# Pooling-group products as three part products, with weights and columns split in the tile's modulation room

## The chip, the cores and the metric

The kernel runs on one core of a Trainium2 chip. The core's engines each work through a queue of their own, in order: TensorE (PE) multiplies, VectorE (DVE) and ScalarE (ACT) work elementwise, GpSimd (POOL) does the same and is almost unused here, SyncE (SP) issues nearly all DMAs. They wait for one another by semaphores. The metric is the device time of one execution in microseconds; lower is better.

## The reference, cut to what matters

One inference step of a two-layer encoder. 1024 prompt rows and 32 sample rows of 1024 channels go through layer 0 (a gating mixer, then a channel MLP, "ffn0") and layer 1 (a pooling mixer, then a channel MLP, "ffn1"). Each half is wrapped in RMS norms, a modulation `rmsnorm(x) * (1 + scale) + shift` and a gated residual. The changed part is the linear map of the pooling mixer:

```python
pooled = jnp.concatenate(outs, axis=-1) - hf[:, L - n_out:]      # window means minus identity
pooled = pooled.astype(h_ext.dtype).reshape(bsz, n_out, POOL_GROUPS, POOL_GROUP_DIM)
y = jnp.einsum('btgc,gcd->btgd', pooled, w_grp).reshape(bsz, n_out, D_MODEL)
return y * scale
```

There are four groups of 256 channels; each has a 256 x 256 matrix. All data are float32.

## The kernel before, in words

Activations lie transposed: 128 channels on the partitions, eight blocks `k` of them, the rows as columns. The rows are cut into three tiles `t` of 384, 384 and 288 columns (the third holds 256 prompt and the 32 sample rows). `acc[t]` is a tile's running array; the residual stream is kept in DRAM (`xd`).

Almost all large products are made of part products. A float32 operand is split in two: `split` (line 1167) writes a first part in the format float32r with ACT (a copy, line 1168) and the rest with DVE (the subtraction runs through the wrapper of line 79). `products` (line 911) then issues three float32r matmuls per pair, first x first, first x second and second x first (lines 916 to 918). Weights stream through three `raw` buffers; ACT writes their first part (line 439) and DVE their second. The products of the pooling groups are the exception: line 1580 multiplies float32 operands directly, `wg` as loaded and `acc` as it is.

A modulated tile is kept as `hh[t]` (first part, ACT, line 889) and `hl[t]` (second part, DVE). Each has one room per tile, tag `h<part><t>`, made by `room` (line 132). The room `hh` of a tile is free between the last up product of ffn0 for that tile and its next modulation, that for ffn1.

The order of the work is written by a planner. `run_ffn` walks through `passes`, a list of (layer, chunk, tiles). In each, `ffn_item` issues four up products per tile (PSUM names `pf`) and later eight down products (`pg`), which DVE adds to `acc`; the first chunk's are copied there by ACT. Between the products `weave` (line 708) streams weights and pulls steps out of `fillers`, generators with the work between two halves of a layer. A step is pulled while the planner's count of DVE time is behind its count of PE time (`tick`, and the wrappers of line 79). What a generator yields says when it may go on: `False` at once, `True` at once and ahead of others, a number only when PE's count has passed the present one by so many microseconds. `pull` looks at the first two fillers. Before the first chunk of a tile, `finish` pulls until that tile's filler is empty, whatever the counts say.

For layer 1 the filler `ffn1_t` (in `to_pool`, line 1445) does, in order: residual and norm behind ffn0; modulation in place; for the third tile the loads and transposes of the cache, and the transposes of the pooling state (`stT`, line 1511), which DVE copies out (`stp`, line 1514); the window sums (`win`) on DVE; then per group a pause, the load of `wg` on SP, four matmuls into two PSUM buffers `pp`, eviction by ACT (line 1584) and squares for the next norm; last `mix_to_ffn` with `residual`, the norm (`pn_r1_1_t`, line 805, with the factors `r` and `q`) and `modulate`. ffn1 runs all of chunks 0 to 3 for the first tile, then for the second, then for the third.

When the kernel is built, the instructions of each engine are put into a fixed order; that order can differ from the one in which the code issued them, and it can be read from the build of either kernel. The engines keep to it.

Of the kernel before, what the change touches and what calls it, by code (L numbers as in the profile page):

```python
# [9 lines left out]
F32 = mybir.dt.float32  # L10
F32R = mybir.dt.float32r
AF = mybir.ActivationFunctionType
ALU = mybir.AluOpType
AX = mybir.AxisListType

P = 128
# [18 lines left out]
def tile_stream_encoder_step(  # L35
# [25 lines left out]
    nc = tc.nc  # L61
    act = nc.scalar.activation
    mm = nc.tensor.matmul
# [5 lines left out]
    def tick(us):  # L69
        time["pe"] += us  # L70
        time["dve"] = max(time["dve"], time["pe"] - 4.0)
# [16 lines left out]
    def pool(name, **kw):  # L88
        return ctx.enter_context(tc.tile_pool(name=name, bufs=1, reuse_waits="tile", **kw))
# [27 lines left out]
        out=quad, in_=ident.rearrange("p (c m) -> p m c", m=32), op=ALU.add, axis=AX.X  # L117
# [9 lines left out]
    def A(t, kb, c0=0, w=None):  # L127
        w = ncol[t] - c0 if w is None else w
        return acc[t][:, kb, HALO + c0 : HALO + c0 + w]


    def room(part, t, name, dtype=F32):
        return work.tile([P, KB, ncol[t]], dtype, tag=f"h{part}{t}", bufs=1, name=name)
# [4 lines left out]
    def ps_dn(name):  # L138
        return psum.tile([P, 512], F32, tag="pd", bufs=3, name=name)

    def ps_ms(name):
        return psum.tile([P, 512], F32, tag="pm", bufs=3, name=name)
# [18 lines left out]
    def t_x(name, shape):  # L161
        return work.tile(shape, F32, tag="x3", bufs=3, name=name)
# [748 lines left out]
    def products(ps, n, terms):  # L911

        last = len(terms) - 1
        tick(3 * len(terms) * (0.004 + n / 2265.0))
        for i, (wh, wl, rh, rl) in enumerate(terms):
            mm(ps[:, :n], wh, rh, start=i == 0, stop=False)  # L916
            mm(ps[:, :n], wh, rl, start=False, stop=False)  # L917
            mm(ps[:, :n], wl, rh, start=False, stop=i == last)  # L918
# [99 lines left out]
    with tc.manual_schedule():  # L1018
# [65 lines left out]
        ps = ps_ms("pv0_5")  # L1084
# [41 lines left out]
    for p, b in v_order:  # L1126
        ps = ps_dn(f"pv{p}_{b}")
# [39 lines left out]
    def split(dst_hi, dst_lo, src, n):  # L1167
        act(out=dst_hi[:, :n], in_=src[:, :n], func=AF.Copy)  # L1168
        tt(out=dst_lo[:, :n], in0=src[:, :n], in1=dst_hi[:, :n].bitcast(F32), op=ALU.subtract)
# [270 lines left out]
    late = pool("late")  # L1440
# [4 lines left out]
    def to_pool(st):  # L1445
        t = st.t
        n = ncol[t]
        npr, nsm = TILES[t][1], TILES[t][2]

        def run():  # L1450
            need_ada(0, 5)
            out = []
# [5 lines left out]
            if nsm:  # L1458
                ext = t_m("ext")
                pool_ext["e"] = ext.rearrange("p (k c) -> p k c", k=KB)  # L1460
                for half in range(2):
# [3 lines left out]
                    for i in range(4):  # L1465
                        k = half * 4 + i
# [9 lines left out]
            for k in range(KB):  # L1476
                for c0, w, v in segs[t]:
                    a = A(t, k, c0, w)
                    stt(
                        out=a,  # L1480
                        in0=a,
                        scalar=coef[:, 1, 0, v, k : k + 1],
                        in1=r[:, c0 : c0 + w],
# [5 lines left out]
                        out=dst,  # L1489
                        in_=a,  # L1490
                        func=AF.Identity,
# [26 lines left out]
            parts = [(acc[t][:, :, 0 : HALO + npr], npr, 0, "p")]  # L1518
            if nsm:
                parts.append((pool_ext["e"], nsm, npr, "s"))  # L1520
            for src, w, dst0, nm in parts:
                for g in range(4):
# [3 lines left out]
                    for lev in range(g + 1):  # L1526
# [3 lines left out]
                            out=nxt[:, :, lo:],  # L1530
                            in0=cur[:, :, lo:],
                            in1=cur[:, :, lo - step : HALO + w - step],
                            op=ALU.add,
# [9 lines left out]
                    if first:  # L1543
                        tt(
                            out=cur[:, :, HALO : HALO + win],
                            in0=cur[:, :, HALO : HALO + win],
                            in1=inv[:, 0:win].unsqueeze(1).broadcast_to([P, 2, win]),
                            op=ALU.mult,
                        )
                        tt(  # L1550
                            out=dst[:, :, 0:win],
                            in0=cur[:, :, HALO : HALO + win],
                            in1=hsrc[:, :, 0:win],
                            op=ALU.subtract,
# [3 lines left out]
                        out=dst[:, :, o:],  # L1558
                        in0=body[:, :, o:],
                        scalar=1.0 / win,  # L1560
                        in1=hsrc[:, :, o:],
# [3 lines left out]
                    yield g != 3  # L1565

            sp = Stat(t, f"rp_{t}")
            for g in range(4):
                yield 0.5
                tick(8 * (0.01 + n / 1220.0))  # L1570
                if g % 2 == 0:
                    wg = t_x(f"wg{t}_{g}", [P, 2, 256])
                else:
                    wg = late.tile([P, 2, 256], F32, tag="wg", bufs=1, name=f"wg{t}_{g}")
                nc.sync.dma_start(wg, pool_w_grp[0, g].rearrange("(k p) d -> p k d", p=P))
                pss = []
                for e in range(2):
                    ps = ps_dn(f"pp{t}_{g}_{e}")
                    for k in range(2):
                        mm(ps[:, :n], wg[:, k, e * P : (e + 1) * P], A(t, 2 * g + k), start=k == 0, stop=k == 1)  # L1580
                    pss.append(ps)
                for e in range(2):
                    d = 2 * g + e
                    act(out=A(t, d), in_=pss[e][:, :n], func=AF.Copy, scale=pscale[:, d : d + 1])
                    sp.square(d)
            yield from mix_to_ffn(sp, 1)

        fillers.append((f"ffn1_{t}", run()))

    def run_ffn(l, after):  # L1590
# [130 lines left out]
```

## Time and profile before

| | |
|---|---|
| time, median of 3 runs | 2165.97 us (2165.47 to 2168.23) |
| the profiled execution's own time | 2166.51 us |
| its span, first to last instruction | 2164.7 us |
| busy: PE, DVE, ACT, POOL | 2147.6, 1421.0, 985.6, 8.0 us |
| pooling products (line 1580), first and last start | 1233.9 and 1565.4 us |
| granted TensorE clock, mean | 0.998 |

The profiled execution is 0.5 us longer than the median of the runs. In the profile a row of a timeline gives start, duration, engine, line and operation with output and inputs, and behind it, where the engine stood idle, for how long and what ended that. In rows of grouped instructions the columns are count, busy time, mean duration in ns, and idle time before them with what ended it. A row of waits gives total, number and longest. A row of a stage gives its length and for each engine the busy time, then the granted clock, the DMA share and GB/s. Durations of matmuls overlap, so the pace of PE is read from their starts. A float32 matmul shows as two passes.

### The profile page before, as it was taken

How to read it: one execution, taken by the hardware profiler on the slowest of the kernel's cores; microseconds unless marked ns; L12 is line 12 of the kernel's file. 1: busy time of each engine (PE TensorE's matmuls, PEld its weight loads, DVE VectorE, ACT ScalarE, POOL GpSimd, SP SyncE). 2: the span in 40 equal slices, each digit the busy share in tenths (PEclk: the TensorE clock that was granted, in tenths of full speed). 3: DMA queues.
4: the chain of work that ended last, by engine and by line, in shares of the span. 5: the costliest groups of instructions: out<-in, count | busy, mean ns of one | idle time of the engine just before them, and what ended most of it. 6: DMA issues, size and time to landing. Idle time of an engine off the chain costs nothing.

```text
span 2164.7 us, 33237 instructions
## 1 busy us (share of the span) xinstructions
PE 2147.6 (99%) x13238; PEld 2082.7 (96%) x13238; DVE 1421.0 (66%) x2517; ACT 985.6 (46%) x1673; POOL 8.0 (0%) x20
## 2 busy tenths in 40 slices
PE   8999999999999999999999999999999999999998
PEld 6878999999999999999999999999999999999998
DVE  6787738467778549576757779869675553523375
ACT  5634322233456652324445566666564542322354
POOL 0000000000000000000000000000000000000000
PEclk9999999999999999999999999999999999999999
DMA  8486524353446444334545466464454541302342
GB/s 296 156 267 210 168 81 135 93 155 103 137 126 218 129 147 146 98 117 140 181 125 164 147 188 202 146 191 156 141 182 134 162 151 59 107 20 69 100 127 108
DMA packets 354864, 312.97 MB, mean 145 GB/s; under 512 B 10834, under 2 KB 316538, under 8 KB 354708
## 3 DMA queue, kind: packets, MB, share of 16 engines
q1 hardware_dynamic: 354452, 310.61, 45.9%
q8 instruction: 104, 1.70, 0.3%
q14 instruction: 52, 0.43, 0.1%
q10 hardware_dynamic: 128, 0.14, 0.0%
q0 software_dynamic: 128, 0.09, 0.0%
HBM read 278.95 MB, written 31.84 MB: 144 GB/s over the span
## 4 chain that ended last, share of the span: by engine, by line
PE 98%; ACT 1%; DMA 0%; DVE 0%; issue 0%; POOL 0%; POOLq 0%; SPq 0%; ACTq 0%; DVEq 0%
PE pf L916 11%; PE pf L918 11%; PE pf L917 11%; PE pg L916 11%; PE pg L918 11%; PE pg L917 11%; PE pu L916 3%; PE pu L918 3%; PE pu L917 3%; PE po L916 3%; PE po L918 3%; PE po L917 3%; PE pv L942 2%; PE pv L944 2%; PE pv L943 2%; PE psp L1262 1%
## 5 line engine op out<-in xcount | busy, mean ns | idle before, releaser
L916 PE MATMUL pg<-fh,wh_dn 128*128 128x384 f32 (+1 forms) x1536 | 496.1, 323 | 0.0
L916 PE MATMUL pf<-hh,wh_up 128*128 128x384 f32 (+1 forms) x1536 | 494.4, 322 | 0.0
L917 PE MATMUL pf<-hl,wh_up 128*128 128x384 f32 (+1 forms) x1536 | 493.1, 321 | 0.0
L918 PE MATMUL pf<-hh,wl_up 128*128 128x384 f32 (+1 forms) x1536 | 493.0, 321 | 0.0
L917 PE MATMUL pg<-fl,wh_dn 128*128 128x384 f32 (+1 forms) x1536 | 492.5, 321 | 0.0
L918 PE MATMUL pg<-fh,wl_dn 128*128 128x384 f32 (+1 forms) x1536 | 492.5, 321 | 0.0
L79 DVE TENSOR_TENSOR wl_up<-raw,wh_up 128x1024 fp32r<-128x1024 f32 x152 | 186.0, 1225 | 170.0 <-ACT wh_up L439 170.0
L916 PEld LDWEIGHTS pg<-fh,wh_dn 128*128 128x128 f32 x1536 | 288.3, 188 | 1.3 <-ACT fh L1168 0.4
L917 PEld LDWEIGHTS pg<-fl,wh_dn 128*128 128x128 f32 x1536 | 288.3, 188 | 1.0 <-DVE fl L79 0.2
L918 PEld LDWEIGHTS pf<-hh,wl_up 128*128 128x128 f32 x1536 | 288.6, 188 | 0.6 <-DVE wl_up L79 0.6
L439 ACT ACTIVATE wh_up<-raw 128x1024 fp32r<-128x1024 f32 x152 | 161.1, 1060 | 280.3 <-PE pf L917 217.2
L917 PEld LDWEIGHTS pf<-hl,wh_up 128*128 128x128 f32 x1536 | 288.3, 188 | 0.4
L916 PEld LDWEIGHTS pf<-hh,wh_up 128*128 128x128 f32 x1536 | 288.2, 188 | 0.4
L918 PEld LDWEIGHTS pg<-fh,wl_dn 128*128 128x128 f32 x1536 | 288.3, 188 | 0.0
L79 DVE TENSOR_TENSOR acc<-acc,pg 128x384 f32<-128x384 f32 (+1 forms) x336 | 174.3, 519 | 154.7 <-PE pg L918 154.1
L439 ACT ACTIVATE wh_dn<-raw 128x1024 fp32r<-128x1024 f32 x152 | 161.0, 1060 | 209.9 <-PE pg L917 174.0
L79 DVE TENSOR_TENSOR wl_dn<-raw,wh_dn 128x1024 fp32r<-128x1024 f32 x152 | 186.1, 1224 | 82.5 <-ACT wh_dn L439 82.2
L79 DVE SCALAR_TENSOR_TENSOR aa<-raw,csil,aa 128x512 f32<-128x512 f32 (+1 forms) x364 | 203.6, 624 | 6.7 <-DMA raw<-in_w_ada_dram 6.3
L1344 ACT ACTIVATE r<-pf 128x384 f32<-128x384 f32 (+1 forms) x192 | 86.6, 451 | 199.3 <-PE pf L918 190.3
L79 DVE TENSOR_TENSOR fl<-r,fh 128x384 fp32r<-128x384 f32 (+1 forms) x192 | 100.4, 523 | 87.2 <-ACT fh L1168 85.8
L916 PE MATMUL pu<-hh,wh_u 128*128 128x384 f32 (+1 forms) x384 | 125.9, 328 | 0.0
L916 PE MATMUL po<-ush,wh_o 128*128 128x384 f32 (+1 forms) x384 | 123.5, 322 | 0.0
(270 smaller groups left out, 2931.7 us busy)
## 6 DMA issues: line engine op xcount, KB each, us to landing
raw<-in_ffn_w_up_dram SPq DMA_DIRECT2D x152, 512.0 KB, 3.9
raw<-in_ffn_w_down_dram SPq DMA_DIRECT2D x152, 512.0 KB, 3.3
raw<-in_w_ada_dram SPq DMA_DIRECT2D x96, 512.0 KB, 4.3
raw<-in_sgu_w_in_dram SPq DMA_DIRECT2D x40, 512.0 KB, 4.1
xd<-acc SPq DMA_DIRECT2D x8, 1536.0 KB, 7.4
raw<-in_sgu_w_out_dram SPq DMA_DIRECT2D x24, 512.0 KB, 3.9
xo_r<-xd SPq DMA_DIRECT2D x32, 384.0 KB, 3.4
vd<-vt SPq DMA_DIRECT2D x32, 256.0 KB, 4.5
```

The lines of the kernel that those rows point to most:

```text
L79: return op(out, *args, **kw)
L439: act(out=wh, in_=r, func=AF.Copy)
L916: mm(ps[:, :n], wh, rh, start=i == 0, stop=False)
L917: mm(ps[:, :n], wh, rl, start=False, stop=False)
L918: mm(ps[:, :n], wl, rh, start=False, stop=i == last)
L942: mm(ps[:m, :], a_h, wh[:, o : o + 512], start=k == 0, stop=False)
L943: mm(ps[:m, :], a_h, wl[:, o : o + 512], start=False, stop=False)
L944: mm(ps[:m, :], a_l, wh[:, o : o + 512], start=False, stop=k == KB - 1)
L1262: mm(sp[:, c * P : (c + 1) * P], vl[:, c, k * P : (k + 1) * P], wr[:, c * P : (c + 1) * P], start=True, stop=True,)
L1344: act(out=r[:, :n], in_=ps[:, :n], func=AF.Relu)
```

## The change

Each group's product is made with `products`, like the rest. The room of `hh[t]` is taken for the pooling stage under the name `pool_t`: 1024 columns hold the group's weights as first and second part (`wh`, `wl`), four pieces of `n` columns hold the two column blocks as first and second parts (`xs`). ACT writes the weights' first part, GpSimd subtracts for the second, ACT and DVE split the columns. The load of `wg` is issued ahead of the pause; behind the splits there is a second pause of 0.8. The line that counted the four float32 matmuls goes away, as `products` counts its own. The two rooms for `wg` stay, with another shape.

```diff
             sp = Stat(t, f"rp_{t}")
+            parts = room("h", t, f"pool_{t}", F32R).rearrange("p k n -> p (k n)")
+            wh, wl = parts[:, 0:512], parts[:, 512:1024]
+            xs = [parts[:, 1024 + i * n : 1024 + (i + 1) * n] for i in range(4)]
             for g in range(4):
+                if g % 2 == 0:
+                    wg = t_x(f"wg{t}_{g}", [P, 512])
+                else:
+                    wg = late.tile([P, 512], F32, tag="wg", bufs=1, name=f"wg{t}_{g}")
+                nc.sync.dma_start(
+                    wg.rearrange("p (k d) -> p k d", k=2),
+                    pool_w_grp[0, g].rearrange("(k p) d -> p k d", p=P),
+                )
                 yield 0.5
-                tick(8 * (0.01 + n / 1220.0))
-                if g % 2 == 0:
-                    wg = t_x(f"wg{t}_{g}", [P, 2, 256])
-                else:
-                    wg = late.tile([P, 2, 256], F32, tag="wg", bufs=1, name=f"wg{t}_{g}")
-                nc.sync.dma_start(wg, pool_w_grp[0, g].rearrange("(k p) d -> p k d", p=P))
+                act(out=wh, in_=wg, func=AF.Copy)
+                nc.gpsimd.tensor_tensor(out=wl, in0=wg, in1=wh.bitcast(F32), op=ALU.subtract)
+                for k in range(2):
+                    split(xs[k], xs[2 + k], A(t, 2 * g + k), n)
+                yield 0.8
                 pss = []
                 for e in range(2):
                     ps = ps_dn(f"pp{t}_{g}_{e}")
-                    for k in range(2):
-                        mm(ps[:, :n], wg[:, k, e * P : (e + 1) * P], A(t, 2 * g + k), start=k == 0, stop=k == 1)
+                    cols = [slice(k * 256 + e * P, k * 256 + e * P + P) for k in range(2)]
+                    products(ps, n, [(wh[:, c], wl[:, c], xs[k], xs[2 + k]) for k, c in enumerate(cols)])
                     pss.append(ps)
```

## The prediction

> **What bounds the kernel now.** I read the page first (its shares of busy time and the chain that ended last), then the waits of PE, then busy time by stage around the pooling products, then the engines' timelines there.
>
> ```profile
> span 2164.7 us, 33237 instructions
> PE 2147.6 (99%) x13238; PEld 2082.7 (96%) x13238; DVE 1421.0 (66%) x2517; ACT 985.6 (46%) x1673; POOL 8.0 (0%) x20
> PE 98%; ACT 1%; DMA 0%; DVE 0%; issue 0%; POOL 0%; POOLq 0%; SPq 0%; ACTq 0%; DVEq 0%
> ...
> PE xT L599 <- DMA x_rows<-in_x_prompt_dram: 4.4, 1, 4.4
> PE pv L987 <- ACT hh L889: 1.8, 2, 1.1
> ...
> 1200.00:1270.00 70.00, 70.00 (x383) 65.75 (x382) 51.49 (x75) 37.72 (x60) 0.00 (x0) 1.00 0.52 153
> 1400.00:1530.00 130.00, 129.96 (x730) 124.31 (x729) 102.37 (x169) 77.22 (x134) 0.00 (x0) 1.00 0.53 166
> ```
>
> TensorE is the bound: 98% of the chain. Its longest waits are in the first 60 us or at the very end; in the two stages that hold most of the pooling products it is never free (70.00 of 70 us, 129.96 of 130). So a microsecond less of PE work there is a microsecond off the end, and a microsecond in which PE stands is one on it. DVE has 18 of 70 and 28 of 130 us free, ACT more.
>
> **The products themselves.** What a group takes on PE is read from starts, because the durations overlap.
>
> ```profile
> 1233.90 2.74 PE L1580 MATMUL pp<-acc,wg 128*128 128x384 f32 x8
> 1236.65 0.34 PE L917 MATMUL pg<-fl,wh_dn 128*128 128x384 f32 x1
> ...
> 1519.71 0.33 PE L917 MATMUL pg<-fl,wh_dn 128*128 128x384 f32 x1
> 1524.56 0.34 PE L918 MATMUL pg<-fh,wl_dn 128*128 128x384 f32 x1
> ...
> 1559.64 2.10 PE L1580 MATMUL pp<-acc,wg 128*128 128x288 f32 x8
> 1561.75 0.34 PE L917 MATMUL pg<-fl,wh_dn 128*128 128x384 f32 x1
> ...
> 2149.77 0.29 PE L918 MATMUL pg<-fh,wl_dn 128*128 128x288 f32 x1
> 2152.53 0.30 PE L918 MATMUL pg<-fh,wl_dn 128*128 128x288 f32 x1
> ```
>
> The second pair of rows lies 28 products apart: 4.85 / 28 = 0.1732 us for a part product of 384 columns; the last pair 21 apart: 2.76 / 21 = 0.1314 for 288. A group of four float32 products shows as 8 passes. With 384 columns it holds PE from 1233.90 to 1236.65, less the one product issued in between: 2.58 us. With 288: 1559.64 to 1561.75 less one, 1.94. The change makes it 12 part products: 12 x 0.1732 = 2.08 and 12 x 0.1314 = 1.58. Two tiles of four groups save 8 x 0.50, the third 4 x 0.36: **5.4 us off PE**.
>
> **The added work on the other engines.**
>
> ```profile
> L1168 ACT ACTIVATE fh<-r 128x384 fp32r<-128x384 f32 x46 | 24.1, 523 | 1.1
> L1424 ACT ACTIVATE xt<-xt 128x512 f32<-128x512 f32 x4 | 2.2, 597 | 2.5 <-DMA xtd<-xt 2.3 <-PE xt L1420 0.2
> ...
> L1650 POOL TENSOR_TENSOR xlast<-zlast,xlast 32x512 f32<-32x512 f32 x2 | 2.5, 1265 | 1581.9 <-ACT zlast L1649 1581.9
> ```
>
> ACT gets 24 column copies at 0.52 and 12 weight copies at 0.60 (the nearest row, 128x512): 20 us. DVE gets 24 subtractions of about the same 0.52: 13 us. GpSimd gets 12 subtractions; the nearest row has 32 partitions, 512 elements each, 1.27 us: 15 us on an engine that is idle. All of it fits in the free time of the 330 us stretch. The 12 weight loads on SP stay 12 and are issued before a pause instead of behind it; what waits for them is now ACT's in-order queue, not PE. I cost them nothing: the copies stand in ACT's queue far behind the load. If that cover went, the rest of a 3 to 4 us transfer would hold ACT's queue, the evictions included.
>
> Inside a group the chain is: evict the group before, copy weights on ACT (0.60), subtract on GpSimd (1.27), third product. In the built order the next group stands 24 products (4.2 us) or more behind the last. One eviction (0.5), a column copy and a square (0.52 each), the second eviction (0.5), the weight copy and GpSimd's subtraction make 3.9 us, from a start about 0.7 us before the group's end. Three groups have just 24 products between; uncovered, they would cost at most 3 x 1.27. The norm's products of the first tile also come closer behind the last group (18 products, 24 before). I take **1 us** for these small waits, 0 to 4.
>
> **What the change moves.** The part that decides lies elsewhere: each group now has two pauses (0.5 and 0.8) instead of one, and the planner counts the subtractions as DVE time, so the chain of a tile runs later. In the built order the second tile suffers. Before, its last norm (`pn_r1_1_1x`) and its modulation stood 241 PE instructions ahead of the first product that reads them. After, they stand right ahead of it. From the two builds' queues (PE, then DVE of the changed kernel, names shortened):
>
> ```
> before PE  8561 pn_r1_1_1x x2   ...   8790 pg1_3_0_7 x12   8802 pf1_0_1_0 x24
> after  PE  8845 pg1_3_0_7 x12   8857 pn_r1_1_1x x2   8859 stT x16   8866..8913 pf1_0_1_0, pf1_0_1_1 mixed, x48   8914 pf1_0_1_2
> after  DVE 1756 acc0+=pg1_3_0_7   1757 stp x2   1759 q   1760 stp   1761 r   1762 wl_dn_24_3   1763 stp
>            1764..1784 14 window operations of tile 2, between them 4 acc1*=r and 3 hl   1785 hl ...
>            1786 acc1*=r x3, hl x3, acc1*=r, 5 small window operations, 1794 hl (the last of 8)
> ```
>
> In the trace of before:
>
> ```profile
> 1487.87 0.34 PE L805 MATMUL pn_r_1x<-sc_r_1x,ones 128*128 128x384 f32 x1
> 1524.74 1.04 PE L1511 MATMUL stT_p<-ident,acc 128*16 128x128 f32 x8
> 1526.49 0.42 PE L916 MATMUL pg<-fh,wh_dn 128*128 128x384 f32 x1
> 1530.76 0.33 PE L916 MATMUL pf<-hh,wh_up 128*128 128x384 f32 x1
> ...
> 1489.49 0.56 DVE L79 SCALAR_TENSOR_TENSOR q_r_1x<-pn_r_1x,q_r_1x 128x384 f32<-128x384 f32 x1 [0.20 <-ACT q_r_1x L810]
> 1491.78 1.14 DVE L79 SCALAR_TENSOR_TENSOR acc<-acc,coef,r_r_1x 128x384 f32<-128x384 f32 x2
> 1492.84 1.22 DVE L79 TENSOR_TENSOR wl_dn<-raw,wh_dn 128x1024 fp32r<-128x1024 f32 x1
> 1506.13 1.14 DVE L79 SCALAR_TENSOR_TENSOR hl<-acc,mod,hh 128x384 fp32r<-128x384 f32 x2
> ...
> 1525.41 1.27 DVE L1514 COPY stp_p<-stT_p 16x512 f32<-16x512 f32 x2
> 1526.60 0.67 DVE L1514 COPY stp_s<-stT_s 16x512 f32<-16x512 f32 x1
> 1527.20 1.20 DVE L79 TENSOR_TENSOR wl_dn<-raw,wh_dn 128x1024 fp32r<-128x1024 f32 x1
> 1528.33 0.67 DVE L1514 COPY stp_s<-stT_s 16x512 f32<-16x512 f32 x1
> 1529.39 1.34 DVE L79 TENSOR_TENSOR win2p<-acc 128x542 f32<-128x542 f32 x2
> 1530.66 0.67 DVE L79 SCALAR_TENSOR_TENSOR acc<-win2p,acc 128x512 f32<-128x512 f32 x1
> 1531.26 0.53 DVE L79 TENSOR_TENSOR acc<-acc,pg 128x384 f32<-128x384 f32 x1
> ...
> 1544.14 0.25 DVE L79 TENSOR_TENSOR win2s<-ext 128x94 f32<-128x94 f32 x1
> 1544.30 0.22 DVE L79 SCALAR_TENSOR_TENSOR acc<-win2s,ext 128x64 f32<-128x64 f32 x1
> ...
> L439 ACT ACTIVATE wh_dn<-raw 128x1024 fp32r<-128x1024 f32 x152 | 161.0, 1060 | 209.9 <-PE pg L917 174.0
> ```
>
> The norm ran at 1487.87, the last second part `hl` ended at 1507.3, the first product came at 1530.76: 23 us to spare. After the change that span of 19 us, or one like it, lies open. Count from 0, when PE is done issuing the last `pg` product:
>
> - PE's own work: 2 norm products 0.35, 16 transposes of the pooling state 1.75 (1524.74 to 1526.49), 48 products 8.31. Sum 10.4 us.
> - DVE reaches `q` 1.62 us behind the norm's start (1487.87 to 1489.49), up to 1.06 later because ACT now has a weight copy in front; I take 2.3. `q` takes 0.5. The third state transposes wait for `q` (three PSUM buffers), half of 1.75 us, so its copy starts at 3.7 and ends at 4.3 (0.60, from 1525.41 and 1526.60). `r` 0.5, the weight's second part 1.13 (1527.20 to 1528.33), the last state copy 0.60: 6.5.
> - Then 10 window sums at 0.63 (1529.39 to 1530.66 for two) and 4 closings at 0.60 (1530.66 to 1531.26): 8.7. Modulation, 16 operations at 0.53 (1491.78 to 1492.84 for two): 8.5. Five small ones at 0.16: 0.8. The last `hl` is there at 24.5; five products (0.87) are left until PE goes on with `pf1_0_1_2`, at 25.4.
>
> PE stands for 25.4 - 10.4 = **15.0 us**. Nothing else is in its queue: `pf1_0_1_2` needs the same eight rows. Bounds: without the window work in front it is 5.5; with every DVE operation at its whole duration instead of its step (0.08 more for some 35) it is 17.8. I take 15.0, since the built order fixes what stands in front.
>
> **The clock.** A PE that starves may come back slow.
>
> ```profile
> 18.55 0.63 PE L987 MATMUL pv<-wh_v,hh 128*128 128x512 f32 x1
> 18.98 0.63 PE L987 MATMUL pv<-wh_v,hl 128*128 128x512 f32 x1
> ...
> 10.00:20.00 10.00, 6.88 (x49) 4.22 (x46) 5.90 (x20) 7.39 (x17) 0.00 (x0) 0.91 1.06 401
> ```
>
> Early in the kernel, where PE waits, the granted clock of a stage is 0.91 and products start 0.43 us apart; 512 columns at the pace of the other rows would take 0.23. A stage of 10 us at 0.91 loses 0.9 us. Two such stages would lose 1.8, part of it while PE starves anyway. I take **1.5**, 0 to 3.5. The Trainium skill (TensorE: Matmul & The Clock Gate, Part 1: The HAM clock gate) says that an idle window of about 3.4 us halves the clock and a busy one restores it. By that rule one half-speed window costs 1.7 us (an estimate from that page); the sum would differ by 0.2, and the half pace above agrees with the rule.
>
> **Sum.** The profiled execution took 2166.51 us: 2166.5 - 5.4 + 15.0 + 1.0 + 1.5 = 2178.6. The median of the runs is 0.5 below that execution, so I predict **2178 us**.
>
> **Rivals.**
>
> 1. *Faster, the saving alone counts:* the modulation of the second tile is ready in time, 2166.0 - 5.4 + 1 = 2161.6. For it: PE never waited here before. Against it: the built order has the norm behind the last `pg` product. It decides only where the stall is under 1.1 us, and 16 modulation operations on DVE alone (8.5) are nearly PE's 10.4. Chance 0.06.
> 2. *No change:* DVE has done the window sums by then, and only norm and modulation are open: 5.5 against 5.4 saved, 2166 to 2167. DVE's free 28 of 130 us speak for it; but the window operations come later in the queue than `pg1_3_0_7`'s accumulation, which waits for PE. Chance 0.06.
> 3. *GpSimd and DVE hold each other up:* if DVE cannot run beside the 12 subtractions, 15 us are shifted between them and the third products of the groups come late; half of it reaching PE gives 2185.5. No row of before has both on SBUF operands at once. The Trainium skill (SBUF — State Buffer, SBUF: two separate sides) says that a GpSimd operation and a DVE operation with two SBUF inputs lock each other out for a whole instruction; no trace so far shows it for this kernel. Chance 0.12.
> 4. *The clock stays at half through the stall:* the 48 products take 8.3 us more: 2186. The granted 0.91, not 0.5, in the early stages speaks against it. Chance 0.06.
>
> **How the numbers follow.** The forecast has 0.70, with its own range 2174 to 2184 (stall 13 to 18, small terms at their ends). Rivals 3 and 4 lie above, 1 and 2 below; a range of 2170 to 2188 leaves out the two low ones and the tail of the third. A difference of 0.2% (4.3 us) is about what a measurement of this kernel tells from none. Faster is rival 1: 0.06. Same is rival 2: 0.06. Slower is the rest: 0.88.
>
> **What would show it.** Steps of 0.17 us in the groups' products and no 8-pass rows: the saving. A wait of PE on `hh` or `hl` of about 15 us in all, just behind the state transposes, with DVE full of window sums there and PE's busy share down in a single stage of some 25 us: the stall. A clock under 1.00 in that stage only: the third term. Waits of PE on GpSimd, or DVE operations that grow beside GpSimd's: rival 3. The prediction is wrong if PE's products for the second tile start without a gap, or if the chain of waits names another place.

## The result

| | before | after |
|---|---|---|
| time, median of 6 runs each, side by side | 2166.72 us (2165.47 to 2168.50) | 2179.42 us (2178.64 to 2180.81) |
| the profiled execution's own time | 2166.51 us | 2180.39 us |
| its span | 2164.7 us | 2178.6 us |

The changed kernel is slower: the ratio is 1.0057, 95% interval 1.0047 to 1.0068. That is 12.7 us on the medians, 13.9 us between the two profiled executions; 2178 had been forecast.

From the page of the changed kernel, its span, the engines' busy time and the chain that ended last by engine:

```profile
span 2178.6 us, 33431 instructions
PE 2150.0 (99%) x13286; PEld 2092.1 (96%) x13286; DVE 1439.0 (66%) x2541; ACT 1000.0 (46%) x1709; POOL 23.7 (1%) x32
PE 94%; DVE 3%; DMA 1%; ACT 1%; issue 1%; POOL 0%; POOLq 0%; DVEq 0%; ACTq 0%
```

The waits of PE in the same execution between 1200 and 1700 us, where all of the change lies (total, number, longest):

```profile
PE pf L916 <- ACT hh L889: 7.0, 2, 5.8
PE pf L917 <- DVE hl L79: 1.8, 2, 1.2
PE pp L917 <- DVE pool L79: 0.9, 1, 0.9
PE pf L916 <- ACT r L1344: 0.8, 1, 0.8
PE stT_s L1511 <- DVE stp_p L1514: 0.4, 1, 0.4
PE pn_r_2x L805 <- ACT xt L1424: 0.4, 1, 0.4
```

In the chain PE gives up 4 points (98 to 94%), and 3 of them go to DVE. The waits that were not there before belong to `hh` and `hl`, that is, to the start of ffn1's second tile. No wait names GpSimd. The same place in the timelines of PE and DVE:

```profile
1526.97 0.34 PE L805 MATMUL pn_r_1x<-sc_r_1x,ones 128*128 128x384 f32 x1
1527.32 1.04 PE L1511 MATMUL stT_p<-ident,acc 128*16 128x128 f32 x8
1528.76 1.20 PE L1511 MATMUL stT_s<-ident,ext 128*16 128x128 f32 x8 [0.40 <-DVE stp_p L1514]
1535.72 1.01 PE L916 MATMUL pf<-hh,wh_up 128*128 128x384 f32 x2 [5.76 <-ACT hh L889]
...
1549.91 0.60 DVE L79 SCALAR_TENSOR_TENSOR hl<-acc,mod,hh 128x384 fp32r<-128x384 f32 x1
1554.02 0.45 PE L916 MATMUL pf<-hh,wh_up 128*128 128x384 f32 x1 [0.83 <-ACT r L1344]
```

And as three stages (length, then busy time of PE, its weight loads, DVE, ACT and POOL, then the granted clock):

```profile
1526.97:1535.72 8.75, 2.59 (x19) 1.45 (x18) 8.25 (x14) 2.57 (x4) 0.00 (x0) 0.85 0.43 126
1535.72:1550.24 14.52, 11.42 (x32) 9.88 (x33) 14.52 (x30) 4.55 (x9) 0.00 (x0) 0.50 0.00 0
1550.24:1554.02 3.78, 2.95 (x18) 2.63 (x17) 2.33 (x10) 1.75 (x4) 0.00 (x0) 1.00 0.00 0
```

The last row of the timeline is `pf1_0_1_2`, the product with which PE goes on at full pace. From the norm to it 27.05 us pass, for 10.4 us of PE work: 16.6 us are lost. The waits in the list make 10.0 of them (7.0, 1.8, 0.8 and 0.4); in nearly all of the rest PE's products follow one another at 0.32 us instead of 0.17. DVE is busy without a gap through the middle stage (14.52 of 14.52), and there the clock stands at 0.50.

The saving is in the starts of a group's twelve products. One group of each width in the changed kernel:

```profile
1243.46 0.33 PE L916 MATMUL pp<-pool 128*128 128x384 f32 x1
1245.37 0.33 PE L918 MATMUL pp<-pool 128*128 128x384 f32 x1
1245.55 0.33 PE L916 MATMUL pf<-hh,wh_up 128*128 128x384 f32 x1
...
1605.16 0.29 PE L916 MATMUL pp<-pool 128*128 128x288 f32 x1
1606.61 0.29 PE L918 MATMUL pp<-pool 128*128 128x288 f32 x1
1606.74 0.34 PE L916 MATMUL pg<-fh,wh_dn 128*128 128x384 f32 x1
```

1243.46 to 1245.55 is 2.09 us, 1605.16 to 1606.74 is 1.58. The account of the two profiled executions: 16.6 lost at the second tile, 1.3 in two small waits (0.9 and 0.4), 5.4 saved: 12.5 of the 13.9. Of the rest, 1.0 is a wait on a weight's second part near 1050 us, ahead of the first PE instruction that the change moves; the kernel before with nothing but a load moved (last experiment) has such a wait there too, 1.3 us, so it is not charged to the change. That kernel also has a wait of 0.4 in front of the third tile's norm, so the 0.4 above may not be the change's either.

### The profile page after: what moved, and what is told of

Its sections match the earlier page's. It is cut to its first block, busy times and chain, and to the rows that moved or that the text cites. A ratio compares the mean times of both kernels' runs of the same rounds, so it can differ in the third digit from the quotient of the medians.

```text
span 2178.6 us, 33431 instructions
## 1 busy us (share of the span) xinstructions
PE 2150.0 (99%) x13286; PEld 2092.1 (96%) x13286; DVE 1439.0 (66%) x2541; ACT 1000.0 (46%) x1709; POOL 23.7 (1%) x32
## 4 chain that ended last, share of the span: by engine, by line
PE 94%; DVE 3%; DMA 1%; ACT 1%; issue 1%; POOL 0%; POOLq 0%; DVEq 0%; ACTq 0%
PE pf L916 11%; PE pf L917 11%; PE pf L918 11%; PE pg L916 11%; PE pg L917 11%; PE pg L918 11%; PE pu L916 3%; PE pu L918 3%; PE pu L917 3%; PE po L916 3%; PE po L918 3%; PE po L917 3%; PE pv L942 2%; PE pv L943 2%; PE pv L944 2%; PE psp L1262 1%
```

## The experiments

The theory: nearly all of the loss comes from the order of the work at the second tile, which the added pause brings about, and the split products themselves save what they were counted to save. Its rivals: the splitting costs (GpSimd against DVE, more on ACT and DVE), or the halved clock does.

**The pause without the part products.** The kernel before, with the second pause added and nothing else:

```diff
                 yield 0.5
+                yield 0.8
                 tick(8 * (0.01 + n / 1220.0))
```

> The kernel before with its float32 products, and the second pause of 0.8 added behind the first: no split, no GpSimd subtraction, no part products. Theory (order): the norm of the second tile again lies right ahead of its first product, though here without the window sums in between, so TensorE loses what q, r and eight modulated blocks on VectorE take beyond its own work, 4 to 8 us, and nothing is saved: 2170 to 2175 us, slower than before. Rival (the splitting itself costs): 2166 to 2167, as before.

Measured: 2174.67 us against 2167.52 of before, ratio 1.0032 (1.0019 to 1.0045). PE's timeline there:

```profile
1533.11 0.34 PE L805 MATMUL pn_r_1x<-sm_r_1x,ones 128*128 128x384 f32 x1
1538.57 1.01 PE L916 MATMUL pf<-hh,wh_up 128*128 128x384 f32 x2 [5.12 <-ACT hh L889]
1540.32 0.52 PE L916 MATMUL pf<-hh,wh_up 128*128 128x384 f32 x1
1542.88 0.52 PE L918 MATMUL pf<-hh,wl_up 128*128 128x384 f32 x1
1543.43 0.33 PE L917 MATMUL pf<-hl,wh_up 128*128 128x384 f32 x1
1543.60 0.34 PE L918 MATMUL pf<-hh,wl_up 128*128 128x384 f32 x1
```

The pause alone makes the kernel slower by 7.1 us on the medians. PE stands for 5.1 us behind the norm, then takes 14 products at steps of 0.32 instead of 0.173: 2.1 more, in all 7.2. The profiled execution is the slowest of its five, 9.7 us above that of before, and its trace has two more waits, 1.0 near 1520 us and 0.9 near 1050 us. So a stall at this place needs neither splits nor GpSimd. It is the stall without the large window sums, which come earlier in this version's order.

**The window sums behind the modulation.** As the changed kernel, but when `finish` forces the second tile, the steps of other fillers that hold the turn are put aside until it is through:

```diff
     def finish(tag):
+        kept = [f for f in sticky if f[0] != tag]
+        sticky[:] = [f for f in sticky if f[0] == tag]
         while any(f[0] == tag for f in fillers):
             pull(True)
+        sticky.extend(kept)
```

> As the changed kernel, but when the second tile's modulation is forced, the third tile's window sums that hold the turn are put back behind it: 10 of the 14 window operations now follow the last hl instead of standing among the modulations. Theory (order, VectorE's queue sets the length of the stall): the stall shrinks by 10 operations of about 0.65 us, 6 to 7 us: 2171 to 2175 us. Rival (the stall is set by TensorE's halved clock or by the splits): the window operations are hidden, 2178 to 2181.

Measured: 2173.65 us, ratio to before 1.0028 (1.0017 to 1.0038), 5.8 us under the changed kernel. The norm starts at 1526.14, and `pf1_0_1_2`, the 49th `pf` product behind it, at 1547.76: 21.6 us instead of 27.05. In DVE's queue nine of the fourteen window operations, not ten as expected, and the five small ones now follow the last `hl`. They had made 5.4 us of the stall, a third of it, and behind the modulation they cause no new wait of PE.

**The subtraction on VectorE.**

```diff
-                nc.gpsimd.tensor_tensor(out=wl, in0=wg, in1=wh.bitcast(F32), op=ALU.subtract)
+                nc.vector.tensor_tensor(out=wl, in0=wg, in1=wh.bitcast(F32), op=ALU.subtract)
```

> As the changed kernel, but the weights' second parts are subtracted by VectorE instead of GpSimd: 12 operations that take GpSimd 1.29 us each go to VectorE at an estimated 0.7 us (its 128x384 split takes 0.544). TensorE's order at the second tile is as in the changed kernel. Theory (order): the stall of 16.6 us stays, so 2177 to 2181 us. Rival (GpSimd and VectorE lock each other out, some 7 us of the loss): that part comes back, 2170 to 2174 us.

Measured: 2178.57 us, ratio to before 1.0056 (1.0043 to 1.0068), the same as the changed kernel's 1.0057. GpSimd's part in the loss is too small to be seen, with intervals that reach some 2.5 us either way. In this trace the half clock ends 20.6 us behind the norm instead of 23.3, and `pf1_0_1_2` comes at 26.06 instead of 27.05.

**Products that fill the stall.** Forty products that nothing reads, right ahead of the second tile's first product:

```diff
                     finish(f"ffn{l}_{t}")
+                    if (l, t) == (1, 1):
+                        fill = ps_ms("fill")
+                        for i in range(40):
+                            mm(fill[:, :384], onesr, hh[0][:, i % KB, :], start=i == 0, stop=i == 39)
                 ffn_item(p, t, after if c == 7 else None)
```

> As the changed kernel, with 40 added products of ones with a block of the first tile's hh, into a spare PSUM buffer that nothing reads, right ahead of the second tile's first product: they take TensorE 6.9 us of the 7 us in which it has nothing to do, and should hold its clock. If the granted clock then stays at 1.00 where it was 0.50 for 14.5 us: theory (the queue of VectorE feeds TensorE so slowly that the clock is worth only its 1.6 us at the end of the stall): 2176.5 to 2178.5 us. Rival (the halved clock sets the length of the stall): 6 to 8 us come back, 2171 to 2173.5 us. If the sparse feed alone lets the clock go to 0.50 again: 2179 to 2180.

Measured: 2179.49 us, ratio 1.0061 (1.0049 to 1.0074). The stages from the norm (1527.70) to `pf1_0_1_2` (1554.70):

```profile
1527.70:1537.68 9.98, 9.57 (x59) 8.59 (x59) 9.48 (x16) 3.20 (x5) 0.00 (x0) 1.00 0.40 110
1537.68:1543.52 5.84, 2.64 (x14) 1.84 (x13) 5.84 (x11) 0.62 (x1) 0.00 (x0) 1.00 0.00 0
1543.52:1550.75 7.23, 6.30 (x19) 5.89 (x20) 7.23 (x18) 3.07 (x6) 0.00 (x0) 0.53 0.00 0
1550.75:1554.70 3.95, 3.12 (x18) 2.80 (x17) 2.57 (x10) 1.99 (x5) 0.00 (x0) 1.00 0.00 0
```

The half clock came later and for half as long (7.2 us at 0.53 instead of 14.5 at 0.50), and the way from the norm to `pf1_0_1_2` is 27.00 us instead of 27.05. The time is that of the third case, in which the sparse feed lets the clock go again, so this run does not decide between theory and rival. To see what the remaining half was worth, 35 more such products were spread behind the first seven blocks of `pf1_0_1_0`, five behind each (`warm` holds their PSUM buffer, for this one product only):

```diff
             mm(ps[:, :n], wl, rh, start=False, stop=i == last)
+            if warm and i < 7:
+                for j in range(5):
+                    mm(warm[0][:, :384], onesr, hh[0][:, j, :], start=False, stop=i == 6 and j == 4)
```

> As the run with 40 added products ahead of the second tile's first product, and 35 more of them spread behind the first seven blocks of it, where TensorE waits for VectorE: its own products and these are 11.3 us of work at full clock in the 12.6 us between the first and the last hl, so they should keep the clock at 1.00 to the end of the stall and delay nothing. With the first 40 alone the clock was at 0.53 for 7.2 us instead of 0.50 for 14.5 us, and the way from the norm to pf1_0_1_2 stayed 27.0 us. Theory (VectorE's queue sets that way whole): 27.0 us again and 2178 to 2180.5 us. Rival (the backlog of some 8 products at the last hl, run through at half clock, is what is left of the clock's price): 25.4 to 26 us, and 2177 to 2178 us.

```profile
1527.40 0.34 PE L805 MATMUL pn_r_1x<-sc_r_1x,ones 128*128 128x384 f32 x1
...
1551.65 0.33 PE L918 MATMUL pf<-hh,wh_up 128*128 128x384 f32 x1
1551.83 0.33 PE L919 MATMUL pf<-hl,wh_up 128*128 128x384 f32 x1
1552.00 0.34 PE L920 MATMUL pf<-hh,wl_up 128*128 128x384 f32 x1
1553.16 0.45 PE L918 MATMUL pf<-hh,wh_up 128*128 128x384 f32 x1 [0.82 <-ACT r L1351]
```

Now PE keeps its full pace to the end (steps of 0.17, granted clock 1.00), and the way is 1553.16 - 1527.40 = 25.76 us: 1.3 us shorter than in the changed kernel. The time, 2178.92 us, ratio 1.0051 (1.0037 to 1.0064), has moved in that direction by less than its interval: the way is the rival's, the time still in the theory's range. So the clock is worth 1.3 us by the trace, which the times alone do not show. What remains, 25.8 - 10.4 = 15.4, is the order, with the 0.82 that `pf1_0_1_2` waits for ACT in it.

**No second pause.**

```diff
-                yield 0.8
+                yield False
```

> The second pause of each group gives way to other work only for one turn of the fillers (the 0.8 becomes False); products, splits and the GpSimd subtraction all stay. Theory (order): the norm of ffn1's second tile comes 186 products ahead of its first product instead of right in front of it, so the stall of 16.6 us goes and the saving of 5.4 us stays; the groups now follow each other after some 13 products (2.2 us), so up to 1 us of waits for split columns or weights per group is to be added: 2161 to 2168 us, below or at the kernel before. Rival (the splitting itself costs: GpSimd and DVE in each other's way, more work on ACT and DVE): the same instructions are all there, so it stays near the changed kernel, 2176 to 2181.

Measured: 2175.31 us, ratio 1.0034 (1.0022 to 1.0047). The stall is gone: the norm lies 180 products and eight transposes ahead, and no wait on `hh` or `hl` is left. But other waits took its place (PE, 1200 to 1700 us):

```profile
PE pp L918 <- POOL pool L1582: 3.0, 5, 0.7
PE pp L916 <- ACT pool L1581: 2.1, 1, 2.1
PE pn_r_2x L805 <- ACT xt L1424: 1.8, 1, 1.8
PE pg L916 <- DVE acc L79: 1.0, 1, 1.0
PE pp L917 <- DVE pool L79: 0.6, 1, 0.6
```

The expectation allowed up to 1 us per group and was still 7 us too low at its upper end. The waits make 8.5 us, the granted clock of 0.93 in the 25 us from 1550 another 1.7; less the 5.4 saved that is 4.8 of the 7.8 by which it is above before, and 3 us stay without a place; the wait near 1050 us that other versions have too makes 0.9 of them.

**No second pause in the first tile alone.**

```diff
-                yield 0.8
+                yield 0.8 if t else False
```

> As the changed kernel, but the second pause is left out in the first tile's four groups alone. Theory (order): the second tile's groups start 132 rows earlier on TensorE, its norm lies 188 products ahead of its first product, and its own groups keep 27 to 85 products between them: no stall, and waits only in the first tile (three gaps of 13 products, under 1 us each): 2161 to 2164 us. Rival (the stall comes from what the second tile does itself, its splits and pauses, which are unchanged): 2176 to 2181.

Measured: 2168.26 us, ratio 1.0002 (0.9993 to 1.0011), no difference from before. The second tile's own code is as in the changed kernel, and its stall is gone; what decides is how late the tile's chain starts. The time is still 4.3 us above the upper end of what was expected, and that lies in the groups. In the third tile, from the timelines of PE and ACT:

```profile
1554.32 0.34 PE L918 MATMUL pg<-fh,wl_dn 128*128 128x384 f32 x1
1555.90 0.40 PE L916 MATMUL pp<-pool 128*128 128x288 f32 x1 [1.25 <-ACT pool L1581]
1557.26 0.40 PE L918 MATMUL pp<-pool 128*128 128x288 f32 x1 [0.82 <-POOL pool L1582]
...
1555.22 0.63 ACT L1581 ACTIVATE pool<-wg 128x512 fp32r<-128x512 f32 x1 [1.93 <-DMA wg<-in_pool_w_grp_dram]
```

Three stages of 2 us there:

```profile
1556.00:1558.00 2.00, 1.18 (x7) 0.94 (x8) 1.17 (x1) 1.18 (x2) 1.21 (x1) 1.00 0.73 260
1558.00:1560.00 2.00, 2.00 (x11) 2.00 (x10) 0.29 (x1) 1.46 (x4) 0.25 (x1) 0.58 0.61 161
1560.00:1562.00 2.00, 2.00 (x9) 2.00 (x8) 1.25 (x3) 1.39 (x5) 1.03 (x1) 0.57 0.85 235
```

ACT waits 1.93 us for the group's weights to land, PE 1.25 for ACT and 0.82 for GpSimd, and when it has work again the clock goes down for 4 us and costs 1.7 more. Three groups of the first tile wait 0.6 us each for GpSimd. All together that is 5.6 us. Both kinds of wait have a remedy.

**Second parts last, and the weights earlier.** On top of the last version, first the products with the weights' second parts behind the group's other eight:

```diff
+                tick(12 * (0.004 + n / 2265.0))
+                cols = [[slice(k * 256 + e * P, k * 256 + e * P + P) for k in range(2)] for e in range(2)]
                 for e in range(2):
                     ps = ps_dn(f"pp{t}_{g}_{e}")
-                    cols = [slice(k * 256 + e * P, k * 256 + e * P + P) for k in range(2)]
-                    products(ps, n, [(wh[:, c], wl[:, c], xs[k], xs[2 + k]) for k, c in enumerate(cols)])
+                    for k, c in enumerate(cols[e]):
+                        mm(ps[:, :n], wh[:, c], xs[k], start=k == 0, stop=False)
+                        mm(ps[:, :n], wh[:, c], xs[2 + k], start=False, stop=False)
                     pss.append(ps)
+                for e in range(2):
+                    for k, c in enumerate(cols[e]):
+                        mm(pss[e][:, :n], wl[:, c], xs[k], start=False, stop=k == 1)
```

> The version without the second pause in the first tile (2168.26), and in each group the four products with the weights' second parts come behind the other eight instead of third in each block, so GpSimd has 8 products (1.4 us) more time instead of 2. That version's trace shows 2.6 us of waits for GpSimd's subtraction in four groups (three of the first tile, one of the third) and 1.2 us for the weights' first part in the third tile. Theory (these waits are what is left between it and the 2162 us expected of it): 2165.5 to 2167 us. Rival (the waits only move to the next thing that is late, the split columns): 2167.5 to 2169.

Measured: 2163.52 us, ratio 0.9985 (0.9976 to 0.9994). No wait of PE on GpSimd is left; of 2.1 us in front of the third tile's first group 0.9 remain, and after that shorter wait the clock stays at 1.00. The time is 2.0 us below the expected range: 4.7 us came back, where only the 2.6 of waits for GpSimd had been counted. With the 0.4 by which the wait for ACT is shorter and the 1.7 of the clock the trace gives the same 4.7. Then the load of each tile's first group ahead of the window sums, into the buffer `wg` that only the odd groups had used (the even and odd groups change buffers; `load(g)` is the load of group `g` as it was):

```diff
+            wg0 = load(0)
             if t == 0:
                 nc.vector.memset(acc[0][:, :, 0:HALO], 0.0)
...
             for g in range(4):
+                wg = load(g) if g else wg0
```

> As the one before, and each tile's first group of weights is loaded ahead of the tile's window sums, into the buffer that nothing else uses. In the third tile ScalarE waited 1.9 us for that load, TensorE then 1.2 us, and the granted clock fell to 0.92 and 0.91 in the 20 us around it. Theory (the load, which the prediction costed at nothing, lies on the path once the pauses are gone): a further 2 to 3 us come back, 2163 to 2165 us, below the kernel before. Rival (the load is not late for the load's place, but for the ring it is queued in): no change to the version before it.

Measured: 2162.15 us against 2167.17 of before, ratio 0.9978 (0.9970 to 0.9987). Its three stages with pooling products:

```profile
1200.00:1270.00 70.00, 69.99 (x403) 68.28 (x403) 54.09 (x82) 42.12 (x73) 7.87 (x4) 1.00 0.51 150
1400.00:1530.00 130.00, 130.00 (x759) 128.75 (x758) 108.07 (x177) 81.36 (x144) 5.23 (x4) 1.00 0.56 170
1530.00:1700.00 170.00, 170.00 (x1052) 169.56 (x1052) 110.06 (x191) 98.55 (x178) 4.25 (x3) 1.00 0.51 156
```

PE does not stand anywhere in them (69.99, 130.00 and 170.00 us). This version is faster than before by 5.0 us, and than the changed kernel by 17. It lies below the range that was expected, but its step from the one before, 1.4 us, is smaller than the 2 to 3 expected and about as large as the scatter of the runs; it lies at the edge of what these runs tell.

**Whose gain it is.** The kernel before with only that earlier load:

```diff
-                if g % 2 == 0:
-                    wg = t_x(f"wg{t}_{g}", [P, 2, 256])
...
+                wg = load(g) if g else wg0
```

> The kernel before, float32 products and single pause, with the one thing added that the fastest version has beside the part products: each tile's first group of weights is loaded ahead of its window sums, into the buffer nothing else uses. Order on TensorE as before. Theory (the 5.0 us by which that version beats the kernel before come from the 48 float32 products turned into 144 part products, 5.4 us on TensorE): 2166 to 2168 us, as the kernel before. Rival (the gain is the earlier load's): 2162 to 2164 us.

Measured: 2167.32 us, ratio 1.0001 (0.9993 to 1.0010). The load alone gives nothing, and PE stands for at most 0.5 us between 1200 and 1700 us both here and in the fastest version; so the 5.0 us belong to the part products, within 0.4 of the 5.4 counted.

## Why the prediction was right, point by point

- *The saving, 5.4:* right. 2.09 and 1.58 us per group were measured for 2.08 and 1.58, and the last two experiments show it as time once nothing stands in its way.
- *The stall, 15.0:* right in place and cause; the size came out with the help of two errors against each other. The last `hl` ended 23.5 us behind the norm's start (24.5 had been counted) and `pf1_0_1_2` came at 27.05 (25.4). The prediction let PE go on five products after the last `hl`; it had to run through a backlog, and `pf1_0_1_2` then waited 0.83 us more for a PSUM buffer's eviction on ACT, which the sum had left out. 16.6 us were lost where stall and clock together had been put at 16.5; with the clock held by added products it was 15.4. The sign that was named, waits on `hh` and `hl` of about 15 us in all, showed as 8.8, because PE filled the rest at half pace. The 241 PE instructions between norm and first product in the kernel before are 252 (228 products and 24 transposes); nothing hangs on it.
- *The clock, 1.5:* 1.3 by the run with the spread products. The size was right and the picture was not, so the size was luck. The term had been drawn from a stage granted 0.91; the clock stood at 0.50 for 14.5 us. It cost little because DVE handed out the operands too slowly for a faster PE: half of that time could be given back without moving the end. What counted was when the half clock ended, since PE then still had products to catch up on: 23.3 and 23.1 us behind the norm the way was 27.05 and 27.00, 20.6 us behind it (the subtraction on VectorE) 26.06, and with no half clock 25.76. The Trainium skill (TensorE: Matmul & The Clock Gate, Part 1: The HAM clock gate) has two clock states, half and full; the stages at 0.50 and 1.00 agree. The prediction's estimate from that page of the Trainium skill, 1.7 us for one half-speed window, is near the 1.3, though for another reason.
- *Small waits, 1:* 0.9 to 1.3 measured, but not at the places the term was made of: GpSimd's subtraction and the first tile's norm made no wait. 0.9 is a wait of the second tile's pooling products on a split column, 0.4 one in front of the third tile's norm, which may not be the change's. That the size fits is luck.
- *The weights' load at nothing:* right for this kernel, and with its condition: the copies stand far behind the load. In the versions without that distance the load's end was on the path, 2.1 us and 1.7 of clock behind it.
- *Rival 1, the saving alone:* needed the stall under 1.1 us; it was 16.6. It is what the fastest version reaches (2162.15 for 2161.6).
- *Rival 2, no change:* needed the window work out of DVE's queue. With nine of the fourteen operations and the small ones behind the modulation the kernel was still 6 us over before. With none in front (the pause without part products) the loss was 7.2, not the 5.5 that this rival counted, since the half clock came on top.
- *Rival 3, GpSimd against DVE:* as a price not seen: no wait of PE names GpSimd, and the subtraction on VectorE changed nothing (2178.57). As a mechanism it is there; see below.
- *Rival 4, half clock through the stall:* its state came about and its price did not. It added the half pace to the stall, where most of it ran in parallel with DVE.

## What to carry to other kernels

A pause in a planner is an instruction to do everything behind it later, for every tile that follows in line; before adding one, read in the built order how far each norm stands ahead of the product that needs it, and what stands in the feeding engine's queue between them. A saving on the bounding engine shows only when that distance holds everywhere: here one pause left out, one product order and one load turned +12.7 us into -5.0 with the same arithmetic. When a pause is taken out, the costs it had been hiding come up: the last transfer, and the slowest engine of the split.

## What the runs showed of the hardware

The granted clock fell after waits of one to two microseconds, and it fell late. Waits of 1.25 and 0.82 us within 3 us (third tile of the version with the pause left out in the first) were followed by 4 us at 0.58 and 0.57, when PE was fully busy again; a single wait of 0.9 us at the same place left it at 1.00. Behind a stand of 5.1 us the half pace lasted 4.6 us of dense work. So 2.1 us of waiting cost 3.8. The Trainium skill (TensorE: Matmul & The Clock Gate, Part 1: The HAM clock gate) says that activity is counted in free-running windows of about 3.4 us. The half pace of 4 and 4.6 us does not contradict that, and no run here can show the windows themselves.

GpSimd's subtraction of 128x512 elements takes 1.28 to 1.34 us in eleven of the changed kernel's twelve groups, and up to three times that beside some of DVE's work. From the timeline of the changed kernel:

```profile
1481.86 1.60 POOL L1582 TENSOR_TENSOR pool<-wg,pool 128x512 fp32r<-128x512 f32 x1 [7.43 <-ACT pool L1581]
1482.69 1.85 DVE L79 TENSOR_TENSOR wl_dn<-raw,wh_dn 128x1024 fp32r<-128x1024 f32 x1
```

From that of the fastest version:

```profile
1265.92 3.99 POOL L1588 TENSOR_TENSOR pool<-wg,pool 128x512 fp32r<-128x512 f32 x1 [17.61 <-ACT pool L1587]
1266.20 1.22 DVE L79 TENSOR_TENSOR wl_up<-raw,wh_up 128x1024 fp32r<-128x1024 f32 x1
...
1268.68 0.55 DVE L79 TENSOR_TENSOR acc<-acc,pg 128x384 f32<-128x384 f32 x1
1269.14 1.09 DVE L79 TENSOR_TENSOR fl<-r,fh 128x288 fp32r<-128x288 f32 x1
```

In the first pair DVE's operation takes 1.85 instead of 1.22 us and ends late; in the second DVE keeps its time and GpSimd's operation lasts 3.99, to 1269.91. Its last 1.29 us begin at 1268.62, just where DVE comes to an operation with one operand in PSUM (`pg`); the next one, `fl`, takes 1.09 us instead of 0.45. The Trainium skill (SBUF — State Buffer, SBUF: two separate sides) says that a DVE operation with two SBUF inputs and a GpSimd operation that reads SBUF block each other for a whole instruction, whichever starts first. These rows agree, with growths of 0.3 to 2.7 us. Nothing waited for the second parts in either case, so it cost nothing here. With eight products in front of the second parts there is room for it; with two and no second pause PE waited for GpSimd even where the subtraction took 1.29 to 1.39 us.
